# Slot rows of two expert pairs from one set of float32r products, with x1 in two parts and 1/rms applied per slot

## The chip, the cores and the metric

The kernel runs on one core of a Trainium2 chip. The metric is the device time of one execution in microseconds (us); lower is better. Three executions of the kernel before were timed, and one more was taken with the hardware profiler, whose rows are shown below. In this text PE is the tensor engine, DVE the vector engine (VectorE), ACT the scalar engine, POOL the GpSimd engine, and SP the engine that does nothing here but issue DMAs.

## What is computed

One layer of a streaming encoder for 256 tokens with 2048 channels, all in f32. A token mixer (pooling, spatial gating, merge gates, output projection) gives `x1 = x + merged @ w_out`. Then comes the hierarchical mixture of experts, the part that the change touches:

```python
h = rmsnorm(x1, g_ffn)                       # 1/rms of each token, times a gain per channel
group = argmax(softmax(h @ w_rg + b_rg))     # 1 of 4 groups
two experts of its 8 by top_k(h @ w_re + b_re), weights = p_group * softmax(top two)
xb = h[tokens of expert e]
hid = silu(xb @ w_g[e]) * (xb @ w_u[e])      # 2048 -> 512, twice
y  += weight * (hid @ w_d[e])                # 512 -> 2048
```

There are 32 experts. At the end a per-layer input is added through a sigmoid gate (`x = x + sigmoid(rmsnorm(x) @ w_ple_gate + b) * (p @ w_ple_up)`), and a last RMSNorm gives the output.

## The kernel before

**Order of the work.** Every weight is read once from HBM into pages in SBUF, and all 256 tokens are worked on at once. First come the dense products of the mixer (to about 530 us). Then x1 is finished, the routing is computed (about 534 to 541 us), and the experts follow in 16 pairs (`NP = 16`, loop over `P` at L1023). The last stage (L1158 on) does three quarters of the down products of pairs 8 to 15 (`FULL = 8`), interleaved with the products of the per-layer gate, and the end.

**The stream of pages.** `Stream` (L40) holds a list of transfers in the order of use and a list of free pages of 128 x 4096 f32 (2048 KB, a double page). When the program says that a page is free (`add`), `pump` (L63) issues the next transfer into it on SP's queue; that transfer waits in SP's queue until the engine that reads the page is done, and what is behind it in SP's queue waits too. `take` hands out pages in the same order. In the expert stage there are four pages in `base` (page0 to 3), three on the right-hand side (pageR, L655), and two made at the start of the expert stage (pageX, L749). `KEEP` (L30) takes one page out of the ring in pair 4 and one in pair 8. In the last pair pages of the right-hand side are not filled again (`retiring`, L1031). pagePT holds the slots' rows `xT` during the expert stage and joins the ring after it (L1091). The first reading of the initial weights is cut into four transfers at L274, each of 256 KB.

**Slots.** An expert takes up to 64 tokens (`CAP`), so a pair has 128 slots. `onehots` (L858) builds, for both blocks of 128 tokens, a matrix of tokens by slots that holds 1/rms of the token where the token has that slot: an equality for the first choice (L861), one more added for the second (L863), a scaling with 1/rms (L865). `dispatch(xt, j)` (L867) forms 4 of the 16 channel groups of the slots' rows: 8 f32 products of the laid-out x1 (`XP`, tile pageM, 128 x 128 as weights) with the one-hots (128 columns), into bank T0 or T1 by `j`, and one DVE operation with the gain (L874). `XP` is filled by `lay` (L677) on ACT, part c after each quarter of the output projection.

**One pair.** `gate_up` (L885) multiplies the slots' rows with the pages of the gate (i = 0) and of the up weights (i = 1), each in parts j = 0 to 3. A part has 4 steps of two products (one expert in each half of the output's partitions); in the profile each f32 product stands as two records, so a part has 16. Two pages serve two parts and are then added to the ring again. Between the parts of i = 0 stand the transposes of the hidden rows (`hidden_t`), the down products (`down_early`) and the scatter (`combine_early`) of the pair before; after each part of i = 1 stands one `dispatch` for the next pair (L1068). Pair 0 has another order (`PARTS`, L28): its own dispatches 0 and 1 ahead of the loop, 2 and 3 between the parts, `late_routing` (L814, with 8 small broadcasts at L847), and the four dispatches of pair 1 after its parts (0, 3), (1, 2) and (1, 3). The slot weights are summed by `slot_weights` (L876); `hidden_gate` (L892) applies the SiLU and `hidden_up` (L896) the second half. After pair 6 stands `overflow` (L954): every engine loads the largest number of tokens of an expert and branches around a body that is for the case that it is over 64 (L962). In front of pair 9 stands `p_up` (L999), the product of the per-layer input, with 32 records at L1012.

**Where x1 and the routing meet.** `inv_rms` (L325) computes 1/rms on POOL. `keep_warm` (L297) fills PE with transposes at the kernel's start (`WARM`, L26) and in the routing.

```python
858  def onehots(s):
         ...
864      for b in range(2):
865          V_.tensor_scalar(OHd[:, b, :], OHd[:, b, :], r1[:, b:b + 1], None, op0=OP.mult)
867  def dispatch(xt, j):
869      ps = (T0, T1)[j % 2].rearrange("p (k s) -> p k s", k=4)
870      for kk in range(4):
871          for b in range(2):
872              mm(ps[:, kk, :], XP[b][:, (4 * j + kk) * 128:(4 * j + kk + 1) * 128], OHd[:, b, :], ...
```

## Time and profile before

| what | value |
|---|---|
| median of 3 runs | 1606.39 us (1606.35 to 1607.93) |
| profiled execution, own time | 1606.54 us |
| its span, first to last instruction | 1604.8 us |
| mean granted clock of PE | 0.986 |
| busy share of the span: PE, DVE, ACT, POOL | 96%, 39%, 26%, 1% |
| moved by DMA | 526.71 MB, mean 328 GB/s |

The span leaves out 1.7 us around the instructions. Busy shares are means over stages that differ, so they tell less than a view by stage. A matmul is pipelined, and its end is modelled, so the spacing of starts tells more than the length of one.

### The profile page before, as it was taken

The page shows a single profiled execution, that of the slowest core. Times are in us where ns is not written, and L with a number is a line of the kernel's source. Part 1 is how long each engine was busy: PE and PEld are TensorE (multiplying, and loading weights), DVE is VectorE, ACT ScalarE, POOL GpSimd, SP SyncE. Part 2 cuts the span into 40 slices and gives each one's busy share as a digit, 9 for nine tenths or more (in the row PEclk, how much of TensorE's full clock was granted, in tenths as well). Part 3 has the DMA queues.
Part 4 walks back from the last instruction along what each step waited for, and adds up shares of the span by engine and source line. Part 5 has one row for each costly group of instructions (what it writes and reads, how often), then busy time and mean ns, then how long its engine had stood idle before and what let it go on. Part 6 is the DMA issues. An engine that isn't in the chain of part 4 may idle for free. (4 is left out here: it accounts for less than half of the span.)

```text
span 1604.8 us, 18479 instructions
## 1 busy us (share of the span) xinstructions
PE 1548.5 (96%) x7525; PEld 920.7 (57%) x7525; DVE 621.8 (39%) x1129; ACT 420.9 (26%) x745; POOL 23.5 (1%) x36
## 2 busy tenths in 40 slices
PE   8999999999999999999999979999999998999994
PEld 7788888888888644344434434434444442456662
DVE  5764565666655312313221212212211121334458
ACT  4644455555455210100000000010000000332244
POOL 0000000000000000000000000000000000000004
PEclk9999999999999999999999989999999999999997
DMA  9655675555674789999999999999999999998881
GB/s 327 229 167 164 217 251 189 184 190 193 231 272 189 284 358 430 426 427 428 427 429 427 428 383 428 423 390 421 421 422 423 422 420 411 392 360 303 290 300 53
DMA packets 133132, 526.71 MB, mean 328 GB/s; under 512 B 16752, under 2 KB 43696, under 8 KB 111024
## 3 DMA queue, kind: packets, MB, share of 16 engines
q1 hardware_dynamic: 119216, 520.12, 82.6%
q10 hardware_dynamic: 13824, 5.34, 1.3%
q8 instruction: 61, 1.00, 0.3%
q14 instruction: 31, 0.25, 0.0%
HBM read 523.33 MB, written 2.10 MB: 327 GB/s over the span
## 5 line engine op out<-in xcount | busy, mean ns | idle before, releaser
L121 DVE TENSOR_TENSOR wlo<-page,whi 128x512 fp32r<-128x512 f32 x362 | 248.8, 691 | 183.4 <-ACT whi L120 179.2
L887 PE MATMUL ps<-page,pagePT 128*64 128x512 f32 x880 | 290.7, 603 | 11.7 <-PEq L962 6.3
L120 ACT ACTIVATE whi<-page 128x512 fp32r<-128x512 f32 x362 | 226.9, 631 | 225.6 <-PE ps L397 112.5
L887 PE MATMUL ps<-pageR,pagePT 128*64 128x512 f32 x768 | 247.7, 608 | 5.5 <-DMA pageR<-in_w_exp_gate_dram 5.0
L395 PE MATMUL ps<-whi,hT 128*128 128x512 f32 x448 | 182.1, 406 | 2.1 <-ACT whi L120 2.1
L397 PE MATMUL ps<-whi,hT 128*128 128x512 f32 x448 | 176.4, 394 | 0.0
L396 PE MATMUL ps<-wlo,hT 128*128 128x512 f32 x448 | 175.8, 392 | 0.4 <-DVE wlo L121 0.4
L911 DVE TENSOR_TENSOR yl<-ps,yh 128x512 fp32r<-128x512 f32 (+2 forms) x72 | 44.7, 629 | 323.5 <-ACT yh L910 323.5
L874 DVE TENSOR_TENSOR pagePT<-ps,gfp 128x512 f32<-128x512 f32 x64 | 44.3, 692 | 300.7 <-PE ps L872 300.7
L887 PEld LDWEIGHTS ps<-page,pagePT 128*64 128x64 f32 x880 | 83.3, 138 | 132.5 <-issue 119.1
L872 PEld LDWEIGHTS ps<-OHd,pageM 128*128 128x128 f32 x1024 | 119.0, 192 | 49.6 <-issue 43.0
L887 PE MATMUL ps<-pageX,pagePT 128*64 128x512 f32 x400 | 138.5, 598 | 0.0
L872 PE MATMUL ps<-OHd,pageM 128*128 128x128 f32 x1024 | 130.8, 281 | 0.0
L887 PEld LDWEIGHTS ps<-pageR,pagePT 128*64 128x64 f32 x768 | 71.1, 138 | 100.8 <-issue 89.2
L910 ACT ACTIVATE yh<-ps 128x512 fp32r<-128x512 f32 (+2 forms) x72 | 39.5, 549 | 334.5 <-PE ps L951 282.0
L395 PEld LDWEIGHTS ps<-whi,hT 128*128 128x128 f32 x448 | 85.0, 190 | 18.8 <-ACT whi L120 2.7
L397 PEld LDWEIGHTS ps<-whi,hT 128*128 128x128 f32 x448 | 84.7, 189 | 18.4
L396 PEld LDWEIGHTS ps<-wlo,hT 128*128 128x128 f32 x448 | 85.2, 190 | 17.4 <-DVE wlo L121 1.1
L944 DVE TENSOR_TENSOR x<-x,ps 128x512 f32<-128x512 f32 x80 | 49.9, 682 | 85.1 <-PE ps L940 85.1
L951 PE MATMUL ps<-page,page 128*64 128x512 f32 (+2 forms) x368 | 69.2, 519 | 0.0
L887 PEld LDWEIGHTS ps<-pageX,pagePT 128*64 128x64 f32 x400 | 39.4, 136 | 49.0 <-issue 47.5
L951 PE MATMUL ps<-page,hTe 128*64 128x512 f32 x208 | 56.1, 592 | 0.0
(262 smaller groups left out, 1674.1 us busy)
## 6 DMA issues: line engine op xcount, KB each, us to landing
page<-in_w_exp_gate_dram SPq DMA_DIRECT2D x27, 2048.0 KB, 20.5
page<-in_w_exp_up_dram SPq DMA_DIRECT2D x27, 2048.0 KB, 19.2
pageR<-in_w_exp_gate_dram SPq DMA_DIRECT2D x25, 2048.0 KB, 22.2
pageR<-in_w_exp_up_dram SPq DMA_DIRECT2D x23, 2048.0 KB, 18.1
page<-in_w_merge_gate_dram SPq DMA_DIRECT2D x32, 1024.0 KB, 5.5
pageX<-in_w_exp_up_dram SPq DMA_DIRECT2D x14, 2048.0 KB, 18.5
page<-in_w_exp_down_dram SPq DMA_DIRECT2D x24, 1024.0 KB, 14.1
page<-in_w_in_dram SPq DMA_DIRECT2D x23, 1024.0 KB, 5.6
```

What stands on the lines that cost most here:

```text
L120: nc.scalar.activation(hi, src, AF.Copy)
L121: nc.vector.tensor_tensor(lo, src, hi.bitcast(F32), op=OP.subtract)
L395: mm(banks[b], ah, hi, start=(k == 0), stop=False, skip_group_check=True)
L396: mm(banks[b], ah, lo, start=False, stop=False, skip_group_check=True)
L397: mm(banks[b], al, hi, start=False, stop=(k == nk - 1), skip_group_check=True)
L872: mm(ps[:, kk, :], XP[b][:, (4 * j + kk) * 128:(4 * j + kk + 1) * 128], OHd[:, b, :], start=(b == 0), stop=(b == 1), skip_group_check=True)
L874: V_.tensor_tensor(xt[j], ps, gfp[:, 4 * j:4 * j + 4, None].to_broadcast([128, 4, 2 * CAP]), op=OP.mult)
L887: mm(acc[i * 64:i * 64 + 64, :], xt[k // 4][:, k % 4, i * CAP:(i + 1) * CAP], ws[i], start=(k == 0), stop=(k == 15), skip_group_check=True)
L910: S_.activation(yh[i][:, 0:w], y[:, 0:w], AF.Copy)
L911: V_.tensor_tensor(yl[i][:, 0:w], y[:, 0:w], yh[i][:, 0:w].bitcast(F32), op=OP.subtract)
L944: V_.tensor_tensor(X2[b][:, cs], X2[b][:, cs], banks[b], op=OP.add)
L951: mm(y[i * 64:i * 64 + 64, :], ht[:, k, i * 64:i * 64 + 64], ws[i], start=(k == 0), stop=(k == 3), skip_group_check=True)
```

## The change

`dispatch` now makes the slots' rows of two pairs at once: the one-hots have 256 columns (4 x 64 slots) of float32r, without 1/rms, and x1 stands in two float32r parts (`hi` and `lo = x1 - hi`), so that each of the 16 products of a `dispatch(j)` has 256 columns and one of four combinations of block and part. Dispatches are made after the parts of i = 1 of odd pairs alone; the four that stood in pair 0 for pair 1 are gone. The rows of both pairs lie in the whole of pagePT, where before two pairs had a half each. 1/rms of each slot is summed like the slot's weight (`slot_scales`) from a row of 1/rms made in `late_routing` by two more broadcasts, and goes into the SiLU's scale and the second half's weight. The low part of x1 is computed on DVE for the first three quarters and on POOL, behind 1/rms, for the last. The two parts take the room of one double page more, so there are two pages on the right-hand side in place of three, and the accumulators of the last stage get tiles of their own. At the start, the first weights come in two transfers in place of four, and four warm-up transposes stand behind the transposes of k = 3 in place of twelve ahead of them. The iota of the slots moves to the expert stage's start.

```diff
-WARM = 12, 12
+WARM = 12, 4
@@ first loads
-            for cut in ((0, 1), (1, 2), (2, 3), (3, 4)) if not off and not i else ((0, 4),):
+            for cut in ((0, 1), (1, 4)) if not off and not i else ((0, 4),):
@@ start, and unit()
-    keep_warm(WARM[1])
...
+                    if k == 3:
+                        keep_warm(WARM[1], PS[6])
@@ end_y()
-                st.passing = [rt.tile([128, 4096], F32, name=f"pageR{i}") for i in range(3)]
-                XP.extend(more.tile([128, 2048], F32, name=f"pageM{i}") for i in range(2))
+                st.passing = [rt.tile([128, 4096], F32, name=f"pageR{i}") for i in range(2)]
+                XP.extend([rt.tile([128, 2048], F32R, name=f"x{n}{i}") for n in "hl"] for i in range(2))
@@ lay(b)
-            S_.activation(XP[b].rearrange("t (k p) -> t k p", k=16)[:, :, 32 * c:32 * c + 32],
-                          X[b][:, cs].rearrange("t (p k) -> t k p", k=16), AF.Copy)
+            hi, lo = (t.rearrange("t (k p) -> t k p", k=16)[:, :, 32 * c:32 * c + 32] for t in XP[b])
+            src = X[b][:, cs].rearrange("t (p k) -> t k p", k=16)
+            S_.activation(hi, src, AF.Copy)
+            if c == 3:
+                last_lo.append(lambda: P_.tensor_tensor(lo, src, hi.bitcast(F32), op=OP.subtract))
+            else:
+                V_.tensor_tensor(lo, src, hi.bitcast(F32), op=OP.subtract)
@@ expert stage
-    OHd = ex.tile([128, 2, 2 * CAP], F32, name="OHd")
+    OHd = ex.tile([128, 2, 4 * CAP], F32R, name="OHd")
+    iot = ex.tile([128, 4, CAP], F32, name="iot")
+    P_.iota(iot, pattern=[[WIN, 4], [1, CAP]], ...
     r1 = inv_rms(ms1, "r1")
+    for f in last_lo:
+        f()
@@ late_routing()
+        for b in range(2):
+            mm(Y1[:, b * 128:b * 128 + 128], r1[:, b:b + 1].to_broadcast([128, 128]), ident, start=True, stop=True)
+        S_.activation(r1row, Y1[:, 0:T], AF.Copy)
@@ onehots(), dispatch()
-        for b in range(2):
-            V_.tensor_scalar(OHd[:, b, :], OHd[:, b, :], r1[:, b:b + 1], None, op0=OP.mult)
...
+    def dispatch(xT, j, n=4 * CAP):
+        for h in range(2):
+            ps = (T0, T1)[h].rearrange("p (k s) -> p k s", k=2)[:, :, 0:n]
+            for kk in range(2):
+                at = (4 * j + 2 * h + kk) * 128
+                for b in range(2):
+                    for part in range(2):
+                        mm(ps[:, kk, :], XP[b][part][:, at:at + 128], OHd[:, b, 0:n],
+                           start=(not b and not part), stop=bool(b and part), skip_group_check=True)
+            k0 = 4 * j + 2 * h
+            V_.tensor_tensor(xT[j][:, 2 * h:2 * h + 2, 0:n], ps, gfp[:, k0:k0 + 2, None].to_broadcast([128, 2, n]), op=OP.mult)
+    def slot_scales(pidc, dst):
+        V_.scalar_tensor_tensor(hid.rearrange("p (a t) -> p a t", a=2), ROW[:, 0:2, :], pidc,
+                                r1row[:, None, :].to_broadcast([128, 2, T]),
+                                op0=OP.is_equal, op1=OP.mult, accum_out=dst)
@@ hidden_gate(), hidden_up()
-        S_.activation(hid_k, acc.rearrange("s (p k) -> s p k", k=4), AF.Silu)
+        S_.activation(hid_k, acc.rearrange("s (p k) -> s p k", k=4), AF.Silu, scale=scale)
+        V_.tensor_tensor(weight, weight, scale, op=OP.mult)
@@ the loop over pairs
-                if (i, j) == (0, 3):
-                    onehots(sq(1))
-                    dispatch(xT[1], 0)
-                if (i, j) == (1, 2):
-                    dispatch(xT[1], 1)
-                if (i, j) == (1, 3):
-                    dispatch(xT[1], 2)
-                    dispatch(xT[1], 3)
-            elif P < NP - 1 and i:
+            elif P % 2 and P < NP - 1 and i:
                 if j == 0:
-                    onehots(sq(P + 1))
-                dispatch(xT[(P + 1) % 2], j)
+                    onehots(lambda i, b: SQ[:, i, b, P // 2 + 1:P // 2 + 2])
+                dispatch(xT, j)
+            if (i, j) == (0, 2):
+                slot_weights(pid[:, P:P + 1], wsl[:, P:P + 1])
+                slot_scales(pid[:, P:P + 1], rsl[:, P:P + 1])
@@ last stage
-    ACC = XP
+    ACC = [fin.tile([128, 2048], F32, name=f"acc{b}") for b in range(2)]
```

The body for the overflow case is changed in the same sense (its rows and weights lie in the kept page, its one-hots have 128 columns).

## Rows read from the trace of the kernel before

**Rows 1.** The page, part 1: busy us, share of the span, instructions

```profile
PE 1548.5 (96%) x7525; PEld 920.7 (57%) x7525; DVE 621.8 (39%) x1129; ACT 420.9 (26%) x745; POOL 23.5 (1%) x36
```

**Rows 2.** Windows over stages: engine busy (instructions), granted PE clock, DMA share, GB/s

```profile
600.00:820.00 220.00, 220.00 (x1108) 95.65 (x1106) 56.19 (x108) 16.32 (x24) 0.00 (x0) 1.00 1.01 428
820.00:940.00 120.00, 108.06 (x516) 46.52 (x514) 28.16 (x54) 8.15 (x12) 0.00 (x0) 0.94 1.01 427
...
1340.00:1420.00 80.00, 72.23 (x311) 31.48 (x308) 23.82 (x46) 20.25 (x37) 0.00 (x0) 1.00 1.04 391
```

**Rows 3.** Waits of PE, whole run: us in total, times, longest

```profile
PE ps L887 <- DMA pageR<-in_w_exp_gate_dram: 5.0, 3, 2.7
...
PE ps L351 <- DMA x<-in_x_dram: 2.0, 2, 1.4
```

**Rows 4.** The chain that ended last, 1178 to 1300 us: start, length, what

```profile
1252.03 3.65 PE ps L887 x14
1255.68 1.98 PE ps L872 x16
...
1288.33 5.34 PE ps L887 x14
```

**Rows 5.** Timeline of PE, last stage: start, length, instruction

```profile
1542.79 0.28 PE L1100 MATMUL ps<-yl,oc 128*128 128x256 f32 x1
1542.90 0.28 PE L1100 MATMUL ps<-yh,oc 128*128 128x256 f32 x1
```

**Rows 6.** Windows around holes of the DMA stream; columns as in rows 2

```profile
544.00:548.00 4.00, 4.00 (x23) 1.60 (x24) 0.69 (x1) 0.00 (x0) 0.00 (x0) 1.00 0.03 8
568.00:574.00 6.00, 6.00 (x36) 3.06 (x34) 0.23 (x1) 0.00 (x0) 0.00 (x0) 1.00 0.52 175
574.00:600.00 26.00, 26.00 (x144) 12.13 (x142) 4.97 (x9) 2.94 (x3) 0.00 (x0) 1.00 0.94 381
944.00:952.00 8.00, 8.00 (x40) 2.88 (x38) 0.00 (x0) 0.00 (x0) 0.00 (x0) 1.00 0.58 225
1060.00:1072.00 12.00, 12.00 (x53) 4.11 (x53) 0.00 (x0) 1.79 (x3) 0.00 (x0) 1.00 0.82 310
1280.00:1300.00 20.00, 18.07 (x72) 5.91 (x70) 3.96 (x11) 1.68 (x2) 0.00 (x0) 0.91 1.01 428
```

**Rows 7.** Timeline of SP's queue, 425 to 760 us: start, length, issues

```profile
453.21 11.78 SPq L67 DMA_DIRECT2D page<-in_w_exp_gate_dram  x2
...
530.99 0.38 SPq L67 DMA_DIRECT2D pageX<-in_w_exp_gate_dram  x1
...
571.77 0.33 SPq L67 DMA_DIRECT2D pageR<-in_w_exp_down_dram  x1
...
582.90 0.33 SPq L67 DMA_DIRECT2D page<-in_w_exp_gate_dram  x1
```

**Rows 8.** Timeline of SP's queue, first 40 us

```profile
1.65 3.97 SPq L282 DMA_DIRECT2D page<-in_w_in_dram  x4
```

**Rows 9.** Groups of instructions by form: count, busy us, mean ns, idle before

```profile
L863 DVE SCALAR_TENSOR_TENSOR OHd<-iot,SQ,OHd 128x128 f32<-128x128 f32 x30 | 9.1, 343 | 0.0
...
L1220 POOL TENSOR_TENSOR pageM<-pageM,page 128x512 f32<-128x512 f32 x6 | 9.3, 1586 | 0.0
...
L1230 DVE TENSOR_TENSOR x<-x,pageM 128x512 f32<-128x512 f32 x8 | 8.6, 1081 | 0.0
...
L883 DVE SCALAR_TENSOR_TENSOR oce<-ROW,pid,oce 128x256 fp32r<-128x256 f32 x16 | 7.7, 484 | 0.6
...
L674 DVE TENSOR_TENSOR x<-x,ps 128x512 f32<-128x512 f32 x8 | 5.4, 682 | 3.1 <-PE ps L397 3.1
```

**Rows 10.** Timeline of SP's queue, 760 to 1100 us

```profile
921.67 0.80 SPq L67 DMA_DIRECT2D page<-in_w_exp_gate_dram  x2
947.58 0.34 SPq L67 DMA_DIRECT2D page<-in_w_exp_up_dram  x1
...
1042.41 19.95 SPq L67 DMA_DIRECT2D page<-in_w_exp_up_dram  x2
```

More of the change, by code (lines that the diff above doesn't have):

```diff
@@ L741, in body @@
     ex = tc.alloc_tile_pool(name="ex", bufs=1, side="left", reuse_waits="tile")
-    xT = [[t[:, j * 512:(j + 1) * 512].rearrange("p (k s) -> p k s", k=4) for j in range(4)] for t in (pg_t, pg_pm)]
+    xT = [pg_pt[:, j * 1024:(j + 1) * 1024].rearrange("p (k s) -> p k s", k=4) for j in range(4)]
     hid = ex.tile([128, 512], F32, name="hid")
-    OHd = ex.tile([128, 2, 2 * CAP], F32, name="OHd")
+    OHd = ex.tile([128, 2, 4 * CAP], F32R, name="OHd")
+    r1row = ex.tile([128, T], F32, name="r1row")
     ROW = ex.tile([128, 4, T], F32, name="ROW")
@@ L749, in body @@
     st.add(*[ex.tile([128, 4096], F32, name=f"pageX{i}") for i in range(2)])
+    iot = ex.tile([128, 4, CAP], F32, name="iot")
+    P_.iota(iot, pattern=[[WIN, 4], [1, CAP]], base=0, channel_multiplier=0, allow_small_or_imprecise_dtypes=True)
     rw = [hid[:, i * 64:(i + 1) * 64].rearrange("p (a e) -> p a e", a=8) for i in range(6)]
@@ L759, in body @@
     dbg("L", [L])
-    keep_warm(ROUTE_WARM[0])
+    keep_warm(ROUTE_WARM[0], PS[4])
     Lg = L[:, :, 0:4]
@@ L811, in body @@
     vsum(SW[:, 1, :], flat(O2))
-    SQ = sm("SQ", [128, 2, 2, NP])
+    SQ = sm("SQ", [128, 2, 2, NP // 2])
     def late_routing():
@@ L952, in down, with overflow @@
                skip_group_check=True)
-    def overflow(ci, xt, ht, spare):
-        xf = xt[0].rearrange("p k s -> p (k s)")
-        rows_of = xf[:, 0:T]
-        wt = [spare[:, i * 512:(i + 1) * 512] for i in range(4)]
+    def overflow(ci, ht, spare):
+        rows_of = spare[:, 1024:1024 + T]
+        wt = [spare[:, i * 512:(i + 1) * 512] for i in range(2)]
+        xt = [spare[:, (4 + j) * 512:(5 + j) * 512].rearrange("p (k s) -> p k s", k=4) for j in range(4)]
         n = sm("ovs", [128, 2, 2])
-        pw = sm("ovp", [128, 2])
+        pw = sm("ovp", [128, 3])
         v = nc.values_load(ci[0:1, 0:1], min_val=0, max_val=T)
@@ L966, in overflow @@
                 with tc.For_i(0, NP, 1) as P:
-                    onehots(lambda i, b: n[:, i, b:b + 1])
+                    onehots(lambda i, b: n[:, i, b:b + 1], 2 * CAP)
                     for j in range(4):
-                        dispatch(xt, j)
+                        dispatch(xt, j, 2 * CAP)
                     slot_weights(pw[:, 0:1], pw[:, 1:2])
+                    slot_scales(pw[:, 0:1], pw[:, 2:3])
                     for acc, wx in ((PS[0], w_exp_gate), (PS[1], w_exp_up)):
@@ L1017, in body @@
     onehots(lambda i, b: SW[:, i, b:b + 1])
-    dispatch(xT[0], 0)
-    dispatch(xT[0], 1)
-    sq = lambda P: (lambda i, b: SQ[:, i, b, P:P + 1])
+    dispatch(xT, 0)
+    dispatch(xT, 1)
+    rsl = sm("rsl", [128, NP])
     late = None
@@ L1039, in body @@
                 at = (j % 2 * 4 + kk) * 512
-                gate_up(acc, xt, 4 * j + kk, [page[:, at:at + 512] for page in pgs])
+                gate_up(acc, xT, P % 2 * 2 * CAP, 4 * j + kk, [page[:, at:at + 512] for page in pgs])
             if j % 2:
@@ L1077, in body @@
             late = None
-            overflow(ci, xt, hT_of(7), st.kept[0])
+            overflow(ci, hT_of(7), st.kept[0])
     late()
```

55 lines of the change are left out of this document (23 added, 32 removed).

## The prediction, made before the changed kernel was run

> **What bounds the kernel now.** I read the page first, then windows over whole stages, then what TensorE (PE) waits for, then the issues of SP's queue one by one. The page has PE busy for 96% of the span [rows 1], which looks like a kernel that PE limits; but a busy PE need not be one at its peak, so the stages decide. In 600 to 820 us the DMA share is 1.01 at 428 GB/s and PE is busy for all of its 220 us; from 820 the DMA share stays at 1.01 while PE begins to have holes; in 1340 to 1420 the DMA share is 1.04 and PE has 7.8 us of holes [rows 2]. The waits agree: PE's longest waits for data are waits for expert pages [rows 3]. So from about 600 to 1400 us the weights arrive at the full rate of the DMA engines, PE first eats a store of pages, catches up near 820, and then follows the arrivals; the last 200 us are PE's own.
>
> From this comes the rule that I use: an edit changes the time only by what it shifts the stream of pages (its position at the start, or the holes in it afterwards), or by what it does before the first page is freed at 548 us, when DMA stands idle for want of a free page, or after 1400.
>
> **The change, part by part.** The sum is made against the profiled execution, 1606.54 us, which is 0.15 above the median of the three runs; so no correction.
>
> *Products of the slots' rows.* Before, each pair has 4 dispatches of 8 f32 products; one takes 1.98 us on PE [rows 4]. After, 8 sets of two pairs have 4 dispatches of 16 float32r products of 256 columns. The nearest row is the float32r products of 256 columns in the last stage, which start 0.11 to 0.12 us apart [rows 5], so one dispatch is 16 x 0.117 = 1.9 us, for two pairs. Of 64 dispatches 32 go: 32 x 2.0 = 64 us of PE. That 256 columns run at this rate is shown by that row, so a failure of the form itself is no case here. Of the 32, 28 lie in pairs 1 to 14 (56 before, 28 after), under the saturated DMA: 28 x 2.0 = 56 us off the path, worth nothing. Cover: a full pair carries 12 pages of 2048 KB, 25.2 MB, 58.8 us at 428 GB/s; without dispatches PE's part of it is shorter still. If that cover were gone the term would be worth up to -64 us (rival 3).
>
> *One double page fewer.* At 544 us nothing moves: DMA share 0.03 [rows 6]. All pages are loaded and wait; from 453.21 to 530.99 there are nine issues of expert pages, the first and the last of which are in [rows 7]. After the change there are eight. From the first release on, the stream is one page later: 2.097 MB / 428 GB/s = **+4.9 us**. Its end arrives 4.9 us later for as long as DMA has no hole, whatever PE does. This is the largest certain term, and it speaks against the change. By the Trainium skill, "DMA: Bandwidth & Descriptors", Specifications, a core gets about 358 GB/s from HBM; the term would then be 5.9 us and the sum 1.0 us more, by my estimate from that figure. The trace shows 428 over 220 us, so the row is used.
>
> *Start of the kernel.* Two DMA issues fewer stand ahead of the second quarter of x, on a queue whose four issues of weights there last 3.97 us, most of it a wait that stays [rows 8]; so the quarter for which PE idles 2.0 us [rows 3] comes two issues, by my estimate 0.8 us, earlier. The warm-up products move behind the fourth transpose and fill part of a wait. -0.7 us; bounds -1.5 (the wait and the slow restart behind it) and 0 (bytes, not issues, are late).
>
> *The routing chain at 534 to 541 us.* PE waits on this chain and DMA has no page, so all of it counts. The one-hots go from six operations on 128 columns to four on 256; L863 takes 343 ns at 128 columns, L883, its like at 256, 484 [rows 9]. 6 x 0.343 and 4 x 0.484 are about equal; I take +0.1 us. The iota of 256 columns moves from the kernel's start to GpSimd's queue just ahead of 1/rms; it can run once the last output products are done, which is before the sums that 1/rms waits for: nothing, or its own length of well under 1 us if it came late. GpSimd gets two subtractions of x1's low part, behind 1/rms on its queue; one on 128x512 takes 1586 ns [rows 9], so they run 3.2 us beside VectorE's chain and end before the first product. What they cost is shared access: L1230 on VectorE takes 1081 ns in the stretch where GpSimd works, a like one (L674) 682 [rows 9]. The chain's operations have 64 elements or fewer: +0.5 us, between 0 and the full 3.2. The other six low parts and the 16 new slot scales lie on VectorE, 39% busy [rows 1], and nothing waits for them soon; were that cover gone, they would cost some 1 us each at L1230's duration. The tiny product ahead of L897 hides under the next pair's first block except at the last pair: +0.15, my estimate.
>
> *Pair 0.* Two more broadcasts in the late routing, of the form of L872, eight of which take 1.98 us [rows 4]: +0.5 us, on the path, because the page release behind them (571.77) comes after DMA has run dry (568 to 574: share 0.52) [rows 6, 7]. Behind that, the four dispatches of pair 1 go, so the next releases (the first is at 582.90) come 3.5 and then 7.5 us earlier, and the holes of 574 to 600 (6% of 26 us) close: -1.6 us [rows 6, 7].
>
> *The stop at the overflow test (L962).* SP issues at 921.67 and then not before 947.58, held by its own branch [rows 10]; DMA runs dry from 944 to 952, 0.42 x 8 = 3.4 us [rows 6]. After the change PE no longer lags, so of the other five pages of a ring of seven all are under way when the last block begins; 7.1 us later 1.45 have landed, two are added: 5.55 pages, 27 us of work, against 24 before. If SP is held as long as now, -2.6 us; bounds -3.4 and 0 (the stop grows with the backlog).
>
> *The per-layer product between pairs 8 and 9.* PE frees no page for 20 us (SP's issue lasts 19.95 us [rows 10]); the hole is 0.18 x 12 = 2.2 us [rows 6]. Ring six: 4 - 1.45 + 2 = 4.55 pages, 22.3 us, against 18 us without the dispatch ahead of it, then one page, then 9.7 us to the next release: a hole of 0.5 us. -1.5; bounds -2.2 and +2 (a page fewer, same pause).
>
> *After the pairs.* The accumulators get tiles of their own where the parts of x1 lay, last read in pair 13. The double pages on the right are retired in the last pair before and after, so four stay. 0.
>
> Sum: 4.9 - 0.7 + 0.1 + 0.5 + 0.15 + 0.5 - 1.6 - 2.6 - 1.5 = -0.25, so **1606.3 us**: no change, although 64 us of PE work go. All favourable ends together: 4.9 - 1.5 + 0.75 - 1.6 - 3.4 - 2.2 = -3.05, 1603.5. All unfavourable: 4.9 + 0 + 3.2 + 0.75 - 1.6 + 0 + 2 = +9.3, 1615.8, which needs three independent bad ends. About 0.2%, 3.2 us, is what a measurement of this kernel can tell from no change.
>
> **Rivals.** (1) *Slower: the page is never paid back.* At 921 us SP's stop grows with the deeper backlog, since each instruction fetch queues behind the pages under way; the hole of 3.4 us stays and that at 1060 too. 4.9 - 0.7 + 0.75 + 0.5 - 1.6 = +3.85, **1610.4**. It decides if SP is held over some 27 us. For it: the hold is 26 us now at a backlog of 24 [rows 10]. Against: only that coincidence speaks for it. (2) *Slower: the clock.* PE will now wait before most blocks. After a wait the first 14 records of a block took 5.34 us against 3.65 elsewhere [rows 4]; the granted clock of 1280 to 1300 is 0.91 [rows 6], so for part of it PE, idle just before, ran at 1.2 in place of 2.4 GHz. With four pages left in the last pair, two are under way in a block, 9.8 us; a block of 7.1 + 1.7 us plus the start of the next transfer overruns that by about 1 us, over three blocks and the serial end: +4 on my sum, **1610.3**. The Trainium skill, "TensorE: Matmul & The Clock Gate", Loop structure matters more than you think, warns of this: a DMA wait between products makes PE go cold. By that rule the change is bad; in the trace the loss is under 2 us each time, and pages under way cover it. (3) *Faster: PE's work counts.* If PE set the pace, 64 us would go: **1542**. The DMA share of 1.01 is against it; what survives is the mild form, every hole closed and the start at its good end: **1603**.
>
> **How the numbers follow.** Forecast (within 0.2%, 1603.2 to 1609.6): 0.54. Rival 1: 0.16, rival 2: 0.08; slower 0.24. Rival 3: mild form 0.20, full form 0.02; faster 0.22. The range, 1602.8 to 1610.8, holds the forecast, the mild form of rival 3 and the two slower ones; outside it lie 2 in 100 at the low end and the heap of bad ends above.
>
> **What would show it.** Right: DMA share near 1.01 from about 575 on; eight issues between 453 and 545; PE's busy share in 650 to 1340 well below now, with tens of us of waits for expert pages from about 665 on; L872's successor with 512 products about 0.117 us apart; the last page of pair 15 landing within 3 us of now; the hole behind the overflow test below 1.5 us. Wrong: DMA share under 0.98 in those stages, a rate other than 428, or a routing chain longer by over 1 us.

## The result: 1.0% slower, and most of it before the first expert page

The changed kernel takes 1622.84 us (median of 4 runs, 1621.11 to 1624.74), the kernel before 1607.16 beside it: a ratio of 1.0097, 95% interval 1.008 to 1.0115. The profiled execution is 1622.31 us long, 15.8 us above that of before.

The page's part 1 of the changed kernel, against [rows 1]:

```profile
PE 1519.7 (94%) x7009; PEld 879.0 (54%) x7009; DVE 633.8 (39%) x1119; ACT 422.6 (26%) x746; POOL 26.6 (2%) x38
```

PE is busy for 28.8 us less and the kernel is 15.8 us longer. The products of the slots' rows went down as the change meant them to: L872 kept PE busy for 130.77 us in the kernel before, L887 for 69.37 us in the changed one, 61.4 us less against the 64 forecast. The stage windows, against [rows 2], show that the stream itself is untouched:

```profile
600.00:820.00 220.00, 208.80 (x966) 86.47 (x964) 57.25 (x104) 16.72 (x24) 0.00 (x0) 0.98 1.01 427
820.00:940.00 120.00, 102.48 (x470) 40.35 (x468) 28.71 (x52) 8.37 (x12) 0.00 (x0) 0.96 1.01 427
1340.00:1420.00 80.00, 68.99 (x278) 28.52 (x274) 21.32 (x42) 16.03 (x30) 0.00 (x0) 0.94 0.98 379
```

From 600 to 940 us the DMA share is 1.01 at 427 GB/s, as before; PE, with less to do, now idles. In 1340 to 1420 us the share falls from 1.04 to 0.98: there is a hole that was not there. PE's waits, against [rows 3]:

```profile
PE ps L909 <- DMA pageX<-in_w_exp_gate_dram: 13.1, 5, 3.2
PE ps L909 <- DMA pageX<-in_w_exp_up_dram: 11.2, 5, 3.9
PE ps L909 <- DMA pageR<-in_w_exp_gate_dram: 10.8, 5, 3.3
```

Where the 15.8 us arise is read best by following one event in both traces. Up to 514 us the event is the n-th split of a block of weights on ScalarE (L120); after that it is the moment at which the stream of weights has moved so many MB. The table gives how much later than in the kernel before each event comes, in us; the columns to the right are experiments, told below.

```
event           before at   after   e1     e4    e5    e13   e14   e16
split 24           48.7      -0.4  -0.2    0.7  -1.0  -0.6   0.7   0.8
split 96          162.1       2.0  -0.2    0.7  -1.0  -0.6   0.7  -0.5
split 200         308.6       6.1  -0.3    0.7  -1.0  -0.6   0.7  -0.5
split 296         441.3       9.9  -0.3    0.7  -1.0  -0.7   0.7  -0.5
split 344         513.6       9.8  -0.3    0.7  -1.1  -0.7   0.7  -0.5
140 MB            619.6      14.6   4.4    5.7   3.7   2.4   3.7  -0.4
260 MB            900.6      14.8   4.3    5.6   3.6   2.2   3.7  -0.3
290 MB            975.3      14.9   4.1    6.0   3.5   2.4  -0.5  -4.2
320 MB           1046.4      14.9   4.0    6.0   3.4   2.3  -0.5  -4.2
340 MB           1097.6      11.6   0.6    8.8   0.1  -1.1  -2.9  -0.6
440 MB           1334.4      11.9   0.6    8.9   0.1  -1.1  -2.9  -0.3
460 MB           1384.1      16.1   5.2   12.3   0.0  -1.2  -3.0   0.5
500 MB           1500.6      15.6   5.0   12.1   0.1  -1.3  -2.5   0.7
520 MB           1602.8      15.6   5.0   12.0  -0.0  -1.3  -2.6   0.6
```

In the column of the changed kernel the largest part is a steady drift of 10 us between 49 and 441 us, in the dense stage, where the change has no line of work. Then come 4.8 us up to 140 MB (the routing chain and the missing page), nothing at the overflow test (260 to 290 MB), -3.3 at the per-layer product (320 to 340 MB) and +4.2 in the last pair (440 to 460 MB).

**The drift.** The groups of zT's products in the dense stage (ns: least, median, most), kernel before:

```profile
L395 PE MATMUL ps<-whi,zT x64: 389/389/390, 213.4 to 422.7; 128*128 128x512 f32 x64
L396 PE MATMUL ps<-wlo,zT x64: 389/389/390, 213.7 to 422.9; 128*128 128x512 f32 x64
```

and the changed kernel:

```profile
L392 PE MATMUL ps<-whi,zT x64: 392/397/401, 216.6 to 432.1; 128*128 128x512 f32 x64
L393 PE MATMUL ps<-wlo,zT x64: 392/397/400, 216.8 to 432.4; 128*128 128x512 f32 x64
```

The same instructions take 397 ns instead of 389, at a granted clock of 1.00 in both (215 to 430 us). The products of hT, which are the most, and of gT do the same; the kernel before, then the changed one, in 60 to 440 us:

```profile
L396 PE MATMUL ps<-wlo,hT 128*128 128x512 f32 x389 | 151.5, 389 | 0.0
L393 PE MATMUL ps<-wlo,hT 128*128 128x512 f32 x389 | 154.2, 396 | 0.0
```

They follow each other every 234 ns instead of 227. In the kernel before seven products start in 1.58 us, in the changed one nine in 2.10 us:

```profile
299.74 0.39 PE L396 MATMUL ps<-wlo,gT 128*128 128x512 f32 x1
...
301.32 0.39 PE L397 MATMUL ps<-whi,gT 128*128 128x512 f32 x1
299.68 0.39 PE L392 MATMUL ps<-whi,gT 128*128 128x512 f32 x1
...
301.78 0.40 PE L392 MATMUL ps<-whi,gT 128*128 128x512 f32 x1
```

Some 1,600 products of hT, zT and gT lie between 49 and 441 us; at 7 ns each that is 11 us, which is the drift. PE waits for nothing there. From 441 to 514 us, where mT takes their place, there is no drift; mT's products in the changed kernel:

```profile
L393 PE MATMUL ps<-wlo,mT 128*128 128x512 f32 x114 | 44.4, 390 | 0.0
```

What differs is where the tiles lie. The change takes 512 bytes per partition (the slot numbers) and some smaller tiles out of the pool at the bottom of the left side, so that x1, the pages, whi, wlo and mT all stand 608 bytes lower, while hT, zT and gT on the right side stay. Before, whi and hT are 49152 bytes apart, which is 24 x 2048; in the changed kernel 49760.

**The routing chain.** VectorE's timeline in the changed kernel (start, length, instruction):

```profile
544.07 0.42 DVE L766 SCALAR_TENSOR_TENSOR L<-ps,r,rb 128x36 f32<-128x36 f32 x2 [1.29 <-PE ps L724]
544.52 0.86 DVE L779 COPY hid<-L 128x64 f32<-128x64 f32 x1
545.42 0.22 DVE L330 TENSOR_REDUCE m<-hid 128x8 f32<-128x64 f32 x1
545.55 0.15 DVE L330 TENSOR_REDUCE gm<-L 128x2 f32<-128x8 f32 x1
545.67 1.22 DVE L782 TENSOR_TENSOR hid<-hid,m 128x64 f32<-128x64 f32 x1
546.82 0.15 DVE L782 TENSOR_TENSOR ohg<-L,gm 128x8 f32<-128x8 f32 x1
```

and GpSimd's beside it:

```profile
543.80 3.02 POOL L682 TENSOR_TENSOR xl<-x,xh 128x512 fp32r<-128x512 f32 x2
```

The copy took 0.19 us before and the comparison 0.22; now the one ends where GpSimd's first subtraction ends, the other where the second ends. From the last load issue of the dense stage to the first page that is freed it is 19.57 us (540.35 to 559.92) instead of 17.59 (530.57 to 548.16): +1.98.

**The holes of the stream.** Windows around them, against [rows 6]; the last line is the new one:

```profile
585.00:611.00 26.00, 26.00 (x126) 8.75 (x124) 2.36 (x4) 1.89 (x4) 0.00 (x0) 1.00 1.00 418
954.00:962.00 8.00, 7.30 (x34) 2.27 (x28) 1.38 (x2) 1.19 (x2) 0.00 (x0) 1.00 0.61 227
1072.00:1084.00 12.00, 12.00 (x56) 4.17 (x58) 1.58 (x3) 1.19 (x2) 0.00 (x0) 1.00 1.00 423
...
1350.00:1358.00 8.00, 8.00 (x38) 4.00 (x38) 2.88 (x7) 1.15 (x1) 0.00 (x0) 1.00 0.58 211
```

The hole behind pair 0 is closed (0.94 before, 1.00 now), that of the per-layer product too (0.82, now 1.00). That of the overflow test is nearly what it was (0.58, now 0.61), and the last pair has lost 0.42 x 8 = 3.4 us. SP's queue ahead of it:

```profile
1327.34 0.33 SPq L67 DMA_DIRECT2D pageX<-in_w_exp_gate_dram  x1
1328.18 0.33 SPq L67 DMA_DIRECT2D pageX<-in_w_exp_up_dram  x1
1337.03 17.50 SPq L67 DMA_DIRECT2D page<-in_w_exp_up_dram  x2
1354.63 0.37 SPq L67 DMA_DIRECT2D pageX<-in_w_exp_up_dram  x1
```

A row marked x2 reaches from the start of the first issue to the end of the second: here one load at 1337 and one at 1354.2, and none between them. The two pages that come free in that time lie on the right side and are no longer refilled.

### The profile page after: what moved, and what is told of

It is laid out like the page before. It is cut to its first block, busy times and chain, and to the rows that moved or that the text cites. A ratio compares the mean times of both kernels' runs of the same rounds, so it can differ in the third digit from the quotient of the medians.

```text
span 1620.5 us, 17459 instructions
## 1 busy us (share of the span) xinstructions
PE 1519.7 (94%) x7009; PEld 879.0 (54%) x7009; DVE 633.8 (39%) x1119; ACT 422.6 (26%) x746; POOL 26.6 (2%) x38
## 5 line engine op out<-in xcount | busy, mean ns | idle before, releaser
L909 PE MATMUL ps<-page,pagePT 128*64 128x512 f32 x912 | 339.9, 609 | 11.9 <-DMA page<-in_w_exp_gate_dram 8.6
L120 ACT ACTIVATE whi<-page 128x512 fp32r<-128x512 f32 x358 | 224.7, 631 | 240.3 <-PE ps L394 207.1
L909 PE MATMUL ps<-pageX,pagePT 128*64 128x512 f32 x576 | 208.8, 622 | 24.3 <-DMA pageX<-in_w_exp_gate_dram 13.1
L909 PE MATMUL ps<-pageR,pagePT 128*64 128x512 f32 x560 | 189.3, 617 | 17.1 <-DMA pageR<-in_w_exp_gate_dram 10.8
L392 PE MATMUL ps<-whi,hT 128*128 128x512 f32 x448 | 184.3, 411 | 1.5 <-ACT whi L120 1.5
L394 PE MATMUL ps<-whi,hT 128*128 128x512 f32 x448 | 178.5, 399 | 0.0
L909 PEld LDWEIGHTS ps<-page,pagePT 128*64 128x64 f32 x912 | 96.9, 139 | 148.3 <-issue 125.5
L909 PEld LDWEIGHTS ps<-pageX,pagePT 128*64 128x64 f32 x576 | 62.7, 142 | 113.8 <-issue 76.5
L909 PEld LDWEIGHTS ps<-pageR,pagePT 128*64 128x64 f32 x560 | 54.4, 141 | 84.2 <-issue 65.1
L920 DVE SCALAR_TENSOR_TENSOR hid<-hid,wsl,ps 128x512 f32<-128x512 f32 x16 | 17.6, 1103 | 150.0 <-PE ps L909 149.2
L887 PE MATMUL ps<-OHd,xh 128*128 128x256 f32 x256 | 65.7, 295 | 0.0
L887 PE MATMUL ps<-OHd,xl 128*128 128x256 f32 x256 | 62.1, 280 | 0.0
```

The source lines that it names most:

```text
L120: nc.scalar.activation(hi, src, AF.Copy)
L392: mm(banks[b], ah, hi, start=(k == 0), stop=False, skip_group_check=True)
L394: mm(banks[b], al, hi, start=False, stop=(k == nk - 1), skip_group_check=True)
L887: mm(ps[:, kk, :], XP[b][part][:, at:at + 128], OHd[:, b, 0:n], start=(not b and not part), stop=bool(b and part), skip_group_check=True)
L909: mm(acc[i * 64:i * 64 + 64, :], xT[k // 4][:, k % 4, at + i * CAP:at + (i + 1) * CAP], ws[i], start=(k == 0), stop=(k == 15), skip_group_ ...
```

## The experiments

Sixteen kernels ran, on one chip per group; "before" was timed beside each group at 1607.4 to 1608.5 us. Ratios are to that, with their 95% intervals. An experiment on the changed kernel begins from e1, which puts the left side back.

### Where the tiles lie: e1, e2, e3, e8, e9

e1, on the changed kernel:

```diff
-    cst.tile([128, 8], F32, name="gap0")
+    cst.tile([128, 160], F32, name="gap0")
```

> The changed kernel with 608 bytes of filler per partition at the bottom of its left side, so that everything above (x1, the pages, the two parts of the weights, mT) stands where it stood before the change; the right side (hT, zT, gT) had never moved. Theory (placement): the 10.5 us by which the changed kernel falls behind between 26 and 441 us come from how far the parts of the weights lie from the transposed activations. Then they vanish: about 1612.3 us, zT's products 389 ns again instead of 396, the lead of 0.7 us from the start still there at 441 us. Rival (the start: the shorter warm-up or the longer second cut leaves TensorE slower): nothing changes, about 1622.8 us and 396 ns.

Measured: 1611.75 us, ratio 1.0025 (1.0016 to 1.0034); 11.1 us less than the changed kernel, zT's products at 389 ns, no drift (column e1).

e2, on the changed kernel, the filler only under the parts of the weights:

```diff
+    spl.tile([128, 152], F32, name="gap1")
     flow = Flow(nc, spl, bg)
```

> The changed kernel with the same 608 bytes put not at the bottom but directly under the parts of the weights, which are released before the expert stage. x1 and the pages stay 608 bytes lower, whi and wlo stand where they stood before the change. If the distance between whi/wlo and hT/zT/gT (moving against stationary operand) is what counts: about 1612.3 us as with the filler at the bottom. If it is where the pages or x1 lie against the right side (what ScalarE and VectorE read for the split): about 1622.8 us.

Measured: 1611.98 us, 1.0027 (1.0016 to 1.0037), 389 ns. Where x1 and the pages lie doesn't matter for the drift.

e3, on the kernel before (three such pairs of lines, for `iot`, `d8` and `qoff`; the new ones stand at the expert stage, each with its iota):

```diff
-    iot = cst.tile([128, 2, CAP], F32, name="iot")
+    iot = ex.tile([128, 2, CAP], F32, name="iot")
```

> The kernel before, with three small tables (608 bytes per partition: the slot numbers, an offset row and a rank row) allocated and filled at the expert stage instead of at the start, and nothing else: the left side lies 608 bytes lower, as in the changed kernel. Theory (placement): the kernel before loses the same 10.5 us by 441 us, about 1617.6 us in all, with zT's products at 396 ns instead of 389. Rival (the start): no change, about 1607 us. The filling of the tables at the expert stage may add up to 1 us to the routing by either.

Measured: 1616.04 us, 1.0059 (1.0041 to 1.0077): 8.7 us lost with none of the change's arithmetic, its products at 397 ns as in the changed kernel:

```profile
L389 PE MATMUL ps<-whi,zT x64: 392/397/400, 215.2 to 430.8; 128*128 128x512 f32 x64
```

e8 and e9 leave the left side 64 and 512 bytes low:

```diff
-    cst.tile([128, 160], F32, name="gap0")
+    cst.tile([128, 144], F32, name="gap0")
...
-    cst.tile([128, 160], F32, name="gap0")
+    cst.tile([128, 32], F32, name="gap0")
```

> The first experiment's kernel with the left side 64 bytes lower instead of 608 (the parts of the weights then lie 64 bytes off a multiple of 2048 from hT, zT and gT). Theory A (any distance that is no multiple costs): zT's products at 396 ns, about 1622 us. Theory B (some larger granule decides): 389 ns, about 1612 us.

> The first experiment's kernel with the left side 512 bytes lower, in place of 64 (where zT's products took 396 ns, as at 608). Theory A (only a distance that is a multiple of 2048, a whole tile row, is fast): 396 ns, about 1620 us. Theory B (a multiple of 512 is enough): 389 ns, about 1612 us.

Measured, one execution each: 1619.97 and 1613.28 us. e8:

```profile
L392 PE MATMUL ps<-whi,zT x64: 393/396/398, 217.1 to 431.9; 128*128 128x512 f32 x64
```

and e9:

```profile
L392 PE MATMUL ps<-whi,zT x64: 389/389/389, 213.1 to 422.3; 128*128 128x512 f32 x64
```

What follows: it matters how far the parts of the weights, which TensorE streams, lie from the tiles that it loads as weights. Counted from a multiple of 2048 bytes, 0 and 512 are fast, 64 and 608 slow by the same 2%. A rule of multiples of 512 would fit these four distances; no other was tried. It is the distance and not the place of whi: mT moved by the same 608 bytes as whi, and its products in the changed kernel kept their rate.

### The page by itself, and the last pair: e4, e5

e4, on the kernel before:

```diff
-                st.passing = [rt.tile([128, 4096], F32, name=f"pageR{i}") for i in range(3)]
+                st.passing = [rt.tile([128, 4096], F32, name=f"pageR{i}") for i in range(2)]
```

> The kernel before with two passing double pages on the right side instead of three, and nothing else: the price of one double page by itself. The prediction's term says +4.9 us, all of it in the stretch from 560 to 900 us, so about 1612. A rival is that the last pair pays as well: with one page fewer the holes in the transfers at 1350 to 1360 us of the changed kernel appear here too, +4 us more, about 1616. By the rival in which TensorE's waits are covered later the price is 0 to 2 us.

Measured: 1618.14 us, 1.0065 (1.0049 to 1.0080), more than either. Column e4 (its start is 0.7 late, which the edit doesn't touch): 5.0 us up to 140 MB, the 4.9 of the prediction; then 2.8 at the per-layer product and 3.4 in the last pair. So a page cost its own length in the stream and once more at two places where the ring runs empty; at a third, the overflow test, it cost only 0.4 us more.

e5, on e1: the pages on the right are refilled as long as the next request is one of the last pair's own.

```diff
-            if passing and self.retiring:
+            if passing and len(self.todo) <= self.tail:
                 continue
...
     down_pages(NP - 1)
+    st.tail = -len(st.todo)
...
     st.want((0, (D,), bcast(b_ple_gate, D)), (2048, (D,), bcast(g_final, D)))
+    st.tail += len(st.todo)
```

> The first experiment's kernel (the change with its left side put back), with one rule altered: the two passing double pages go on being refilled in the last pair as long as the next request is one that this pair itself consumes, instead of being retired from its start. Theory (the hole of the last pair comes from the refill order: with six pages instead of seven the two retired ones are the first that come free, and the pair's last requests wait for the four others): the jump of 4.5 us at 450 MB of the stream goes, about 1607.2 us. Rival (the hole comes from TensorE's clock or from the pair's own work): no change, 1611.7 us.

Measured: 1607.02 us, 0.9993 (0.9983 to 1.0003). The jump at 460 MB is gone, and the window of the hole, which in e1 reads

```profile
1341.00:1349.00 8.00, 8.00 (x40) 2.78 (x38) 1.15 (x5) 1.16 (x1) 0.00 (x0) 1.00 0.62 242
```

reads in e5

```profile
1341.00:1349.00 8.00, 8.00 (x40) 2.75 (x38) 0.70 (x3) 1.17 (x1) 0.00 (x0) 1.00 0.99 422
```

The two pages are now loaded in that place:

```profile
1325.80 3.36 SPq L67 DMA_DIRECT2D pageR<-in_w_exp_up_dram  x2
```

The granted clock, 0.72 at 1349 to 1361 us in e1, is 1.00 at 1347 to 1359 us in e5, so the slow clock came with the hole. Freed of its two accidents, the change takes the time of the kernel before.

### TensorE's saved work: e7

On e1:

```diff
                     onehots(lambda i, b: SQ[:, i, b, P // 2 + 1:P // 2 + 2])
-                dispatch(xT, j)
```

> The first experiment's kernel without any dispatch after the first pair's: 28 sets of 16 products and their scalings are left out, so that the slots' rows of pairs 2 to 15 are those of pairs 0 and 1. It takes some 55 us of TensorE's time out of the span. Theory (the stream of weights sets the time): 0 to 3 us faster, 1609 to 1612. Rival (TensorE's work counts): 10 us faster or more, 1602 or less.

Measured: 1611.37 us, 1.0018 (1.0008 to 1.0028), 0.4 us less than e1. The window of e1

```profile
600.00:820.00 220.00, 207.74 (x958) 84.36 (x954) 57.21 (x104) 16.51 (x24) 0.00 (x0) 0.98 1.01 428
```

becomes

```profile
600.00:820.00 220.00, 195.20 (x825) 69.11 (x820) 45.52 (x88) 15.80 (x23) 0.00 (x0) 0.97 1.01 428
```

133 products fewer in it, 12.5 us more idle time, the same 428 GB/s. Over the whole run the products of the slots' rows fall from 69.6 to 8.6 us. TensorE's work in the pairs is worth nothing while the stream is full.

### The routing chain: e6, e11, e13

e6, on e1 (`times` and the copy likewise):

```diff
     def eq(o, x, y):
-        V_.tensor_tensor(o, x, y, op=OP.is_equal)
+        V_.scalar_tensor_tensor(o, x, 1.0, y, op0=OP.mult, op1=OP.is_equal)
```

> The first experiment's kernel with the routing's copy, comparisons and products on VectorE written in the three-operand form (times 1 or 0, then the operation) and nothing else. In the changed kernel one copy took 0.86 us instead of 0.19 and one comparison 1.23 instead of 0.22, each ending when a subtraction of GpSimd ended; the three-operand L beside them took 0.41 for two as before. Theory (only some forms of VectorE instruction wait for GpSimd): both are back at about 0.22, the routing chain is 1.7 us shorter, about 1610.0 us in all. Rival (each instruction waits for GpSimd whatever its form, or the read of the same rows is what is slow): no change, 1611.7 us.

Measured: 1611.86 us, 1.0023 (1.0013 to 1.0033): a miss. The three-operand form waits as well:

```profile
533.81 0.90 DVE L779 SCALAR_TENSOR_TENSOR hid<-L 128x64 f32<-128x64 f32 x1
...
534.99 1.20 DVE L783 SCALAR_TENSOR_TENSOR hid<-hid,m 128x64 f32<-128x64 f32 x1
```

GpSimd's two subtractions beside it:

```profile
533.09 3.02 POOL L682 TENSOR_TENSOR xl<-x,xh 128x512 fp32r<-128x512 f32 x2
```

Both instructions of VectorE have two inputs in SBUF, as has the comparison of the changed kernel. L766, which reads one of its inputs from PSUM, and the reductions, which have a single one, don't wait. The number of inputs isn't all, since the copy of the changed kernel has one and waited. The Trainium skill, "SBUF — State Buffer", SBUF: two separate sides, says that VectorE and GpSimd share a pair of ports that one instruction holds to its end, and that a VectorE instruction with two SBUF inputs, or in a two-port mode, needs it; the trace agrees, with 0.90 us for a form that takes 0.2 alone, ending some 0.1 us after GpSimd's. The copy would have to be the second of these cases; no run shows in which mode it ran.

e11, on e5: the last low parts go to VectorE behind the first one-hots, and the first dispatch makes the high parts' products first.

```diff
-                last_lo.append(lambda: P_.tensor_tensor(lo, src, hi.bitcast(F32), op=OP.subtract))
+                last_lo.append(lambda: V_.tensor_tensor(lo, src, hi.bitcast(F32), op=OP.subtract))
...
     onehots(lambda i, b: SW[:, i, b:b + 1])
-    dispatch(xT, 0)
+    for f in last_lo:
+        f()
+    dispatch_first(xT)
```

> The kernel with late retiring (1607.0 us) with the last two low parts of x1 taken from GpSimd and put on VectorE behind the first one-hots; the first dispatch makes all its products with the high parts first. The subtractions then lie 2.1 us long on the path, of which some 0.9 us runs beside the first eight products; against that, two instructions of the routing no longer wait 1.7 us for GpSimd. Theory (the two waits are GpSimd's doing): both instructions at about 0.2 us, the routing chain 1.7 us shorter, and 0.5 to 1.1 us gained in all, 1605.9 to 1606.5. Rival (the waits have another cause): they stay, and the kernel is 1 us slower, 1608.

Measured: 1607.60 us, 0.9997 (0.9988 to 1.0006): no gain, though the copy is back at 0.20 us. From the last load issue to the first page freed it is 19.26 us (529.88 to 549.14) against 19.58 in e5 (529.44 to 549.02). The waits were GpSimd's doing, and what they cost went into the subtraction, which the eight products don't cover. (In this kernel and in e12 the first dispatch's sums lose some products of the high parts, because a bank is started twice between them; its time has all the instructions.)

e13, on e5, does both first dispatches together, in four banks with one start each: 32 products with the high parts, then 32 with the low parts.

```diff
-    dispatch(xT, 0)
-    dispatch(xT, 1)
+    for f in last_lo:
+        f()
+    dispatch_first()
```

> The kernel with late retiring (1607.0 us) with the last two low parts of x1 on VectorE, behind the first one-hots, and the first two dispatches run together in four banks: all products with the high parts first (some 1.9 us), then those with the low parts. VectorE's 2.0 us of subtraction then lie beside TensorE's 1.9 us. Theory (two instructions of the routing wait for GpSimd, 1.7 us in all, and that is the whole price of the low parts): the first page is freed 1.3 to 1.7 us earlier and the kernel takes about 1605.5 us. Rival (the subtraction only moves): 1607.

Measured: 1605.99 us, 0.9985 (0.9976 to 0.9994). VectorE's timeline:

```profile
533.99 0.20 DVE L779 COPY hid<-L 128x64 f32<-128x64 f32 x1
...
534.48 0.23 DVE L782 TENSOR_TENSOR hid<-hid,m 128x64 f32<-128x64 f32 x1
...
539.98 2.01 DVE L684 TENSOR_TENSOR xl<-x,xh 128x512 fp32r<-128x512 f32 x2
```

From the last load issue to the first page freed it is now 17.93 us (529.82 to 547.75), 1.64 less than in the changed kernel; the two instructions alone are 0.66 and 0.99 us shorter. So 1.64 of the 1.98 us were GpSimd's subtractions.

### The overflow test: e10, e12, e14, e15, e16

e10, on e5:

```diff
-            overflow(ci, hT_of(7), st.kept[0])
```

> The kernel with late retiring (1607.0 us) without the test for overflowing experts and the branch behind it, which is left out with all that it would run; nothing takes the branch with these inputs. In every kernel so far SP issues nothing for 23 to 28 us there and comes back 1.0 to 1.6 us after the last page under way has begun its last transfers. Theory (SP is held until the stream has run dry, however long that is, so no number of pages closes the hole): the hole of 3.4 us at 940 to 948 goes and TensorE's pause of 6.5 us at 920 with it, about 1603.6 us. Rival (the pages' arrival is late for another reason there): 1607.0.

Measured: 1614.36 us, 1.0039 (1.0026 to 1.0052), slower, while the hole is gone (4.3 us between 270 and 290 MB). It lost 10.1 us ahead of 120 MB: two small tiles went with the call, the left side stood 64 bytes lower, zT's products took 396 ns. e15 puts 64 bytes of filler back (`gap0` of 176 columns).

> The kernel with late retiring without the test for overflowing experts, again, but with the 64 bytes of the small tiles that went with it put back as filler. The first such kernel lost 10.1 us by 450 us and won 4.3 at the stop. Theory (its loss was the placement of the left side, 64 bytes off): about 1607.0 - 4.3 = 1602.7 us, zT's products at 389 ns. Rival (something else that leaving out the test did): 1613 to 1614 us again.

Measured: 1605.02 us, 0.9981 (0.9972 to 0.9991): the placement was the cause, and the stop is worth some 4.4 us at its place, of which 0.7 is lost again by 340 MB and about 1 in the last stage.

e12, on e11, issues the first five loads behind the test from ScalarE's queue.

```diff
-                self.nc.sync.dma_start(self.at(page, off, shape), src)
+                (self.nc.scalar if self.other > 0 else self.nc.sync).dma_start(self.at(page, off, shape), src)
+            self.other -= 1
```

> The kernel with the last low parts on VectorE, and the first five loads behind the overflow branch issued from ScalarE's queue instead of SP's. TensorE is held only 6.5 us by that branch, SP until the stream is dry. Theory A (the hold belongs to SP, whose own queue carries the stream): ScalarE is back within 10 us, the hole at 940 to 948 us shrinks from 3.4 us to below 1, and the kernel gains 2.5 to 3.4 us on the one before. Theory B (each engine that hardly works there fetches its code behind the pages under way): ScalarE is held as long, no gain or a loss of up to 2 us.

Measured: 1616.28 us, 1.0050 (1.0035 to 1.0066). This is 8.7 us over e11, more than either theory allows. ScalarE, done at 922.2, issues its first load at 946.86, about as late as SP in e5 (946.42):

```profile
921.62 0.60 ACT L938 ACTIVATE hTe<-ps 128x512 f32<-128x512 f32 x1 [16.35 <-PE ps L937]
946.86 0.34 ACTq L68 DMA_DIRECT2D pageR<-in_w_exp_gate_dram  x1
```

That looks like the second theory, and isn't. (The hole here is no longer than in e11: DMA share 0.67 against 0.65 in 940 to 950 us. The loss comes later: TensorE waits 7.3 us for one page, until 989.9 us, and the stream runs at a share of 0.74 and 0.83 from 990 to 1010. Why that page comes late was not tried.) In the program the branch that runs here makes SP wait on each of the eight counts of its loads until all loads issued have landed, and adds to them what the other branch would have; ScalarE's loads wait on the same counts. The eight waits stand in the traces, on the line of the branch; here are those of the kernel before and of the changed one:

```profile
L962 SPq EVENT_SEMAPHORE  x8: 17/17/17, 942.1 to 947.4; - x8
L985 SPq EVENT_SEMAPHORE  x8: 17/17/17, 937.7 to 957.2; - x8
```

e14, on e13, takes the waits away from SP, at the two loads inside `overflow`:

```diff
-                                nc.sync.dma_start(ws[i], wv[ds(P, 1), i, k].rearrange("q p c -> (q p) c"))
+                                P_.dma_start(ws[i], wv[ds(P, 1), i, k].rearrange("q p c -> (q p) c"))
```

> The kernel of the run beside this one (last low parts behind the one-hots), with the loads inside the overflow branch issued from GpSimd's queue instead of SP's. In the program, the side of the branch that is taken here makes SP wait until each of the eight counts of its loads has reached all that was issued before, because the other side would raise them; with the loads on GpSimd these waits are no longer SP's. Theory A (it is these waits that hold SP until the stream is dry): SP issues again within 10 us of its branch, the hole at 940 to 948 us goes, 3.4 to 4.3 us gained on the run beside it, about 1601.5 us. Theory B (SP fetches its code behind the pages under way): SP is held some 27 us as before and nothing is gained.

Measured: 1604.20 us, 0.9980 (0.9971 to 0.9989), the fastest of all: 3.6 us under before in the same group, 18.6 under the changed kernel. SP at the stop, in the changed kernel:

```profile
930.50 27.17 SPq L67 DMA_DIRECT2D pageR<-in_w_exp_gate_dram  x2
957.81 0.34 SPq L67 DMA_DIRECT2D page<-in_w_exp_up_dram  x1
```

and in e14, with the windows of its stream under it:

```profile
918.71 18.22 SPq L67 DMA_DIRECT2D pageR<-in_w_exp_gate_dram  x2
937.05 0.63 SPq L67 DMA_DIRECT2D page<-in_w_exp_up_dram  x1
```

```profile
940.00:945.00 5.00, 5.00 (x27) 1.72 (x24) 0.00 (x0) 0.00 (x0) 0.00 (x0) 1.00 1.01 429
945.00:950.00 5.00, 5.00 (x26) 1.85 (x23) 1.36 (x2) 1.19 (x2) 0.00 (x0) 1.00 0.99 421
```

On the line of the branch SP now has one instruction, and no wait:

```profile
L999 SPq COMPARE_BRANCH  x1: 50/50/50, 920.0 to 920.0; - x1
```

The 18.22 us of its row are no stop of this kind: 16.5 of them are a wait of the next load for a page that TensorE still reads, and the pages under way outlast it. The second theory would have left the stop as it was. Column e14 gains 4.2 us there and gives 1.0 back, against e13, at the per-layer product; the whole gain on e13 is 1.8 us, half of what was expected.

e16 is the same edit on the kernel before.

> The kernel before with the loads inside the overflow branch issued from GpSimd's queue instead of SP's, and nothing else. Theory A (SP's waits in the branch hold the stream): the hole of 3.4 us at 944 to 952 us goes here too, about 1604 us. Theory B (code behind the pages): no change, 1607.5.

Measured: 1606.30 us, 0.9986 (0.9976 to 0.9996). The hole closes here too (column e16, 3.9 us), but the per-layer product takes 3.6 back. There the kernel before has its dispatches in TensorE's way, which may be the reason; no run tries it alone. What the runs show as a whole, 1.5 us, is less than half of e14's 3.6.

## Why the prediction was wrong

Forecast: no change, 1606.3 us, in a range up to 1610.8; measured: 1622.84 us. Two terms that the sum put at nothing make nearly all of the difference: the first and the last of this list.

- **A term that the sum did not have.** The prediction's rule, that all counts which the change does before the first page is freed, held. But its list had only the start and the routing chain there, and no term for the dense products between them. It costed the moved iota as an instruction on GpSimd's queue ("nothing, or its own length"), and that instruction did cost nothing: it took 0.36 us on GpSimd at 540.62, 2 us ahead of 1/rms. The moved thing that cost was the tile: 512 of the 608 bytes by which the left side sank. e1 and e3 show it from both sides: 11.1 us go with it and 8.7 us come with it. The row that could have warned is not one of the trace: two tiles named `gap` in the kernel before, which do nothing but set distances.
- *Products of the slots' rows* off the path worth nothing: right (e7, 0.4 us for 61 us of work). One dispatch of two pairs takes 69.37 / 32 = 2.17 us in place of 1.9, which changes nothing.
- *One double page fewer*, +4.9: right where it was put (5.0 in e4), but the page by itself costs again at two later places (2.8 and 3.4 in e4); the prediction had the first as a bound of +2 and the second not at all.
- *Start*, -0.7: the split at 48.7 us comes 0.4 earlier; in four other kernels with the same start it comes between 1.0 earlier and 0.7 later, so the size is not settled.
- *Routing chain*: the mechanism right, the size off. 0.6 forecast, bound 3.2, measured 1.98, 1.64 of it GpSimd's (e13). The row of an instruction on 512 elements beside GpSimd was no measure for small ones: each waits for the end of GpSimd's instruction, however short it is itself.
- *Pair 0* (+0.5, -1.6) and the page together: +3.8 forecast from the first freed page on, +2.8 measured. The hole closed, and more.
- *The stop at the overflow test*, -2.6: failed. The prediction reckoned with SP held for a time of its own, so that pages under way would cover it. The bound of 0, a stop that grows with the backlog, is what came: SP is held until the last of the pages has landed (e14), so more pages under way make the stop longer and leave the hole (3.1 us here, 3.4 before). The eight waits at L962 stood in the trace of the kernel before.
- *The per-layer product*, -1.5: -3.3 in the trace. The page alone would have cost 2.8 there (e4). e16, where the dispatches stay, shows the same place taking back what an earlier stream had won.
- *After the pairs*, 0, "so four stay": failed, +4.2. Four pages stay, but six come to that place in another order, and two of those in use were retired while the pair's own requests were still open (e5). Rival 2 had the place and the size (+4), but not the cause. TensorE does run at a granted clock of 0.72 in 1362 to 1374 us, behind a wait that the hole made; e5 touches only which pages are filled again, and hole, slow clock and loss go together.

Rival 1 was right that the hole stays, but not with its reason, the fetch of instructions (e14), and wrong about the rest. Without the placement and the last pair (e5) the change takes 1607.0 us, 0.7 above the forecast; the two accidents, 11 and 4.7 us, were what the sum didn't contain. That the rest comes so close is in part luck: the stop and the routing chain came out 2.7 and 1.4 us worse than forecast, the per-layer product and the page with pair 0 1.8 and 1.0 us better, and these misses nearly cancel.

## What to carry to other kernels

When an edit adds, drops or resizes a tile, look at what lies above it in its pool before costing any instruction: compare the addresses of what TensorE streams with those of what it loads, and keep their distance. A page of a ring can have a price again where the ring runs empty, not only in the steady stream, and a page that is to be given up can serve until the last request that ends before it goes. And where a queue stands still, list its instructions at that line and ask which waits the program put there, before explaining it by the chip.

## What the runs showed of the hardware

- A float32r product of 512 columns follows its predecessor after 227 ns or 234, by the distance between the tile it streams and the tile it loads: fast at 0 and 512 bytes from a multiple of 2048, slow at 64 and 608 (e1, e9; e8, changed kernel). Why is open; only these four distances were tried.
- An instruction of 64 elements on VectorE that takes 0.2 us alone took up to 1.23 us beside a subtraction on GpSimd, whether copy, comparison or three-operand form; reductions beside it kept their 0.15 to 0.22 us (changed kernel, e1, e6).
- A second start in a bank between the parts of the first sum there seems to spoil that sum: the output of e11, which has such starts, is off by 0.11 (relative), that of e13, with one start per bank, is right. The order of the products differs too, so the start alone is not shown.
- TensorE is held 6.1 to 6.9 us by the overflow branch in each kernel that has it (6.3 before, 6.1 in e11, 6.9 in e12), also in e14 (6.4), where SP's waits are gone; what holds it there was not tried.
